# A two-layer decoder trunk on one core: ordering the vector work of the down projection, and its first leftover tile by weight rows

## The chip, the cores and the metric

The kernel runs on one core of one Trainium2 chip. The metric is the device time of one execution in microseconds (us); the time before is the median of three runs. TensorE (PE in the profile) multiplies into eight PSUM banks, VectorE (DVE) and ScalarE (ACT) read those banks, GpSimd (POOL) works from SBUF only, and SyncE (SP) issues most DMAs. Each engine works through its own queue in order and waits on semaphores for the others.

## The reference

A decoder trunk over 1040 tokens (16 meta tokens and 1024 of the input), width 1024, two layers. Layer 0 is a state-space mixer, layer 1 an attention over keys and values that are projected once; each is followed by a convolutional gated feed-forward block. The parts that matter here, cut from the reference:

```python
def _conv_ffn(u, w_up, conv_w, conv_b, w_down):
    h = _causal_dwconv(u @ w_up, conv_w, conv_b)
    g, val = jnp.split(h, 2, axis=-1)
    return (jax.nn.silu(g) * val) @ w_down
...
        if layer < n_a:
            h = h + _ssd_mixer(_rmsnorm(h, ssd_norm[layer]), ...)
        else:
            if layer == n_a:
                kv = _rmsnorm(h, kv_norm) @ w_kv
            ...
            h = h + o @ sb_w_o[j]
        h = h + _conv_ffn(_rmsnorm(h, ffn_norm[layer]), ffn_w_up[layer], ffn_conv_w[layer],
                          ffn_conv_b[layer], ffn_w_down[layer])
    return _rmsnorm(h, final_norm)[:, N_META:]
```

The feed-forward width is 2816, which is 22 rows of 128 weights in the down projection.

## The kernel before

Every float32 product is made of three fast matmuls (`mm3`, L168): each operand is split into a high part (a ScalarE copy) and a low part (the operand minus the high part, on VectorE or GpSimd), and high by high, high by low and low by high are added up in PSUM. So each operand costs one ScalarE and one subtraction before TensorE can use it.

The stages follow one another: mixer, output projection (`out_proj`), entry to the feed-forward block (`enter_ffn`), up projection (`up`), down projection (`down`), attention (`attention`), its projection (`o_proj`), and the second feed-forward block. Outside the attention and part of the mixer, a planner at build time sets each engine's order: it walks through the program with its own durations, and puts an instruction that it thinks is ready ahead of an earlier one that it thinks is not. Inside `manual_schedule` blocks (the attention, L1565) the order is that of the program.

**The down projection** (`down`, L993) runs once per layer. Its first 16 weight rows are multiplied by a seven-product scheme for 2x2 blocks: in each of two rounds the seven products come in the order 1, 2, 7, 6, 5, 3, 4 (L1077), each in two halves (x = 0, 1), so there are 28 steps. `make(n)` (L1133) prepares the operands of step n one step ahead by `Set.operands` (L1033). For products 7, 6, 5 and 3 a weight difference is formed in place, for 7, 6, 5 and 4 a token difference (L1039 to L1050, all on VectorE). Then come the high part of the weights on ScalarE (L1054), their low part on GpSimd (L1055), the high part of the tokens on ScalarE (L1056) and their low part on VectorE (L1057). The buffers of the token parts are of a pool of 28 (`qp`), of which some three steps' worth are free. A step is 48 matmuls in layer 0 (two token tiles of 260 columns, four output blocks) and 24 matmuls of 512 columns in layer 1. A finished product is moved out of its PSUM banks by `add` (L1099): L1103 on ScalarE for some products of the first round, L1105 on VectorE for the others. In the kernel before, only the differences of product 7 are tied to something: they stand behind the last instruction of the up projection (`behind_up`).

The last six weight rows are plain products, four token tiles (j = 0 to 3) by eight output blocks f (L1172 to L1186). `accumulate` (L396) runs all six rows into one bank and adds the bank to h on VectorE (L403); its banks come from a cycle of five. The seven products are put together by 28 VectorE additions (`sums`, L1069, L1074), two of which are asked for behind each block of tile 0. `weights` (L1110; L1113 on ScalarE, L1114 on GpSimd) and `tokens` (L1117; L1124, L1125) prepare the operands.

**The entry to layer 0's feed-forward block**: `out_proj` (L728) adds the last four rows of the mixer's projection inside `enter_ffn`, in four token tiles. Their right-hand operands are split for both halves of the tokens (`split_half`, L185; L189 on ScalarE, L190 on VectorE) before the first tile.

**The last normalization of layer 0**: `norm` (L249) is called for three token tiles; it splits h (L273, L274), adds up squares (`square_sum`, L231) and calls `rstd` (L198), which sums over partitions by two matmuls with a matrix of ones (L204) and makes the factors on ScalarE and VectorE (L207 to L212). The attention then begins with the projections of keys and queries (`half`, L1231) of tiles 0 and 1.

Of the kernel before, what the change touches and what calls it, by code (L numbers as in the profile page):

```python
# [8 lines left out]
F32 = mybir.dt.float32  # L9
# [4 lines left out]
P = 128  # L14
D = 1024
KD = D // P
# [9 lines left out]
HALO = 4  # L26
# [34 lines left out]
PAIRS = 8  # L61
# [25 lines left out]
class Trunk:  # L87
# [161 lines left out]
    def norm(self, h, j, u):  # L249

        s0, n = TT[j]
        if u is None:
            u = [(self.Q("uh", F32R), self.Q("ul", F32R)) for _ in range(KD)] + [self.rp.tile([P, QW], F32, tag="r", name=self.nm("r"))]
        rows = [h[k][:, s0 : s0 + n] for k in range(KD)]
        for k in range(KD):
            self.parts(rows[k], u[k], s0, n, None, self.nc.gpsimd if (j, k) in LPOOL else self.nc.vector)
        self.rstd(self.square_sum(rows, n, D), n, D, u[KD][:, HALO + s0 : HALO + s0 + n], j == 0)
        return u

    def scaled_project(self, w, u, j, q=None, bank=None):  # L260
# [467 lines left out]
    def out_proj(self, hd, ys, yd, pool):  # L728

        a = self.a  # L730
        h = [None] * KD
        for g in range(3):
            ops = [self.split(ys[g][q] if yd[g] is None else self.fetch(yd[g][q], "y"), "y") for q in range(4)]
            for f in range(KD):
                w = self.load_w(a["w_out_f"][g, f], 4 * P)
                if g == 0:
                    h[f] = self.fetch(hd[f], "h", front=HB)
                for s0, n in TT:
                    self.accumulate(h, f, s0, n, lambda i, f: (w[0][:, i * P : i * P + P], w[1][:, i * P : i * P + P]), ops, HB)
        half = lambda x: [self.split_half(ys[3][q][:, L // 2 * x : L // 2 * (x + 1)], "y") for q in range(4)]  # L740
        first = half(0)
        ws = [self.load_wd(a["w_out"][12 + i], i < 2) for i in range(4)]
        return self.enter_ffn(0, h, [(ws, first), (ws, half(1))], pool)

    def load_wd(self, src, row):

# [2 lines left out]
    def enter_ffn(self, layer, h, last, pool):  # L749


        nc, g = self.nc, FFN[layer]
        FN, S = g.tile, g.half
        r = self.rp.tile([P, QW], F32, tag="r", name=self.nm("r"))
        if not g.lead:
            nc.gpsimd.tensor_copy(r[:, :HB], self.zero[:, :HB])
        d = self.dp.tile([KD, P, g.n], F32, tag=f"hm{layer}", name=f"hm{layer}")
        banks = cycle((self.mm, self.lg, self.ex, self.mm, self.lg))
        ms = {}

        def tile(j, work):
            ws, ops = last[j // 2]
            ms[j] = self.sm("ms")
            for f in range(KD):
                self.accumulate(h, f, *g.span(j), lambda i, f: (ws[i][0][:, f * P : f * P + P], ws[i][1][:, f * P : f * P + P]), ops, HB, next(banks), g.part(j // 2)[0])
                self.square_row(ms[j], h, f, *g.span(j))
                next(work, None)

        def factors(j):

            s0, n = g.span(j)
            c = r[:, HB + s0 : HB + s0 + n]
            b, ps = self.tmp("y")[:, :n], ms.pop(j)[:, :n]
            if j % 2 == 0:
# [12 lines left out]
        def form_tiles():  # L787

            out = {}

            def own(i):
                hl = self.Q("bh", F32R), self.Q("bl", F32R)
                out[i] = [tuple(x[:, k * FW : k * FW + HB + FN] for x in hl) for k in range(KD // 2)]

            def wide():
                wide = [(self.Q("bh", F32R), self.Q("bl", F32R)) for _ in range(KD // 4)]

                for x in wide[1]:
# [12 lines left out]
        w0 = self.up_weights(layer, 0, pool)  # L811
        ws0 = next(w0)
        for j in (0, 1):
            tile(j, iter(()))
            factors(j)
        store(0)
        forms = [form_tiles()]
        work = self.forms(layer, h, r, 0, forms[0], pool)
        for j in (2, 3):
            tile(j, work)  # L820
            factors(j)
        store(1)
        for _ in work:
            pass
        return d, ws0 + next(w0), forms, rest()
# [167 lines left out]
    def down(self, layer, gd, hd, pool, after, each=None):  # L993
# [3 lines left out]
        nc, a = self.nc, self.a  # L997
# [8 lines left out]
            nosync = mybir.DependencyInfo(mybir.DependencyClass.NoSync, mybir.DependencyReason.DATA)  # L1006
            self.tc.add_manual_dep(ins.ins, other.ins.name, nosync, reason=reason)

        def behind_up(ins):

            behind(ins, self.last_up, "behind the up projection")

        def pair(t, w):
            return t[:, : 2 * w].rearrange("p (q c) -> p q c", q=2)
# [1 line left out]
        class Set:  # L1016
# [16 lines left out]
            def operands(me, i):  # L1033

                b, w = me.b, me.w
                b11, b12, b21, b22 = b[0, 0], b[0, 1], b[1, 0], b[1, 1]
                a11, a12, a21, a22 = w[0, 0], w[0, 1], w[1, 0], w[1, 1]
                if i == 7:
                    behind_up(tt(a21, a11, a21, op=SUB))  # L1039
                    behind_up(tt(b12, b22, b12, op=SUB))  # L1040
                elif i == 6:
                    tt(a21, a22, a21, op=SUB)
                    tt(b11, b11, b12, op=ADD)
                elif i == 5:
                    tt(a11, a11, a21, op=ADD)
                    tt(b12, b22, b11, op=SUB)
                elif i == 3:
                    tt(a21, a12, a21, op=SUB)
                elif i == 4:
                    tt(b11, b21, b11, op=SUB)  # L1050
                x, y = {1: (b11, a11), 7: (b12, a21), 6: (b11, a21), 5: (b12, a11), 3: (b22, a21), 4: (b11, a22), 2: (b21, a12)}[i]
                gh, gl = (pair(self.Q(z, F32R), QW // 2)[:, :, :S] for z in ("gh", "gl"))
                wh, wl = (self.wp.tile([P, 1024], F32R, tag=z, name=self.nm(z)) for z in ("wh", "wl"))
                nc.scalar.activation(wh, y, AF.Copy)  # L1054
                pt(wl, y, wh.bitcast(F32), op=SUB)  # L1055
                nc.scalar.activation(gh, x, AF.Copy)  # L1056
                tt(gl, x, gh.bitcast(F32), op=SUB)  # L1057
                return gh, gl, wh, wl

        kinds = (self.mm, self.sm, self.lg, self.sm, self.mm, self.sm, self.lg, self.ex)  # L1060
# [110 lines left out]
        res, work = None, sums()  # L1171
        for j in range(4):  # L1172
            out = h if j > 1 else h[:4] + h22
            for f in range(KD):
                self.accumulate(out, f, FN * j, FN, lambda i, f: (ws[i][0][:, f * P : f * P + P], ws[i][1][:, f * P : f * P + P]), us[j // 2], bank=next(banks), base=S * (j // 2))
                for _ in range(2 if j == 0 else 1):
                    next(work, None)
                if j == 3 and each:
                    each(h, f)
            if j == 0:  # L1180
                tokens(1)
            else:
                if j == 1:
                    for f in range(4):
                        tt(acc[5, f], acc[5, f], h22[f], op=ADD)
                res = after(h, j - 1, res)  # L1186
# [184 lines left out]
    def attention(self, u, pool):  # L1371
# [30 lines left out]
        for kind, j in (("k", 0), ("q", 0), ("k", 1), ("q", 1)):  # L1402
            for h in range(2):
                for f in first.half(kind, j, h):
                    f()
        self.token_factors(u[KD], pool)
        for p in range(PAIRS):
            prev = None
# [24 lines left out]
    def o_proj(self, hd, od, pool):  # L1433
# [24 lines left out]
                self.accumulate(h, f, *g.span(j), lambda i, f: (w[0][:, i * P : i * P + P], w[1][:, i * P : i * P + P]), ops[j // 2], HB, base=-g.lead)  # L1458
        ops = [part(p, 0) for p in range(first, PAIRS)]
        ws = [self.load_wd(a["w_o"][first - 2 + i], i < 2) for i in range(4)]  # L1460
        return self.enter_ffn(1, h, [(ws[2:], ops), (ws, [part(p, 1) for p in range(first - 2, PAIRS)])], pool)


    def finish(self, h, j):
# [168 lines left out]
```

## Time and profile before

| what | value |
|---|---|
| median of three runs | 2992.21 us (2991.93 to 2997.83) |
| the profiled execution | 2995.8 us, span of its instructions 2994.1 us |
| granted TensorE clock, mean | 0.983 |
| TensorE busy | 2879.0 us, 96% |
| VectorE busy | 2304.0 us, 77% |
| ScalarE, GpSimd busy | 1653.4 us, 1308.0 us |

In the span of the profiled execution, layer 0's entry to the feed-forward block begins at about 837 us, its down projection runs from about 1363 to 1614 us, the attention from there to about 2165 us, and layer 1's down projection from about 2735 us to the end. A wait's row names the engine and line that waited, what it waited for, the sum in us, the number of waits, and the longest.

### The profile page before, as it was taken

How to read it: one execution, taken by the hardware profiler on the slowest of the kernel's cores; microseconds unless marked ns; L12 is line 12 of the kernel's file. 1: busy time of each engine (PE TensorE's matmuls, PEld its weight loads, DVE VectorE, ACT ScalarE, POOL GpSimd, SP SyncE). 2: the span in 40 equal slices, each digit the busy share in tenths (PEclk: the TensorE clock that was granted, in tenths of full speed). 3: DMA queues.
4: the chain of work that ended last, by engine and by line, in shares of the span. 5: the costliest groups of instructions: out<-in, count | busy, mean ns of one | idle time of the engine just before them, and what ended most of it. 6: DMA issues, size and time to landing. Idle time of an engine off the chain costs nothing.

```text
span 2994.1 us, 57318 instructions
## 1 busy us (share of the span) xinstructions
PE 2879.0 (96%) x21863; PEld 2738.0 (91%) x21863; DVE 2304.0 (77%) x4026; ACT 1653.4 (55%) x3403; POOL 1308.0 (44%) x1250
## 2 busy tenths in 40 slices
PE   7999999989998999999999999999899999999998
PEld 4999898879998999998999999999798999998878
DVE  5586868885369887878876888888839878878785
ACT  4555555553245555555334788887736555554433
POOL 1254444442334666663442222222342766764451
PEclk9999999999999999999999999999999999999999
DMA  5233333323122222224232122221331222225321
GB/s 162 70 107 90 106 89 105 106 70 139 63 80 72 79 73 84 79 86 177 74 130 86 55 61 66 64 70 54 106 141 57 80 84 78 75 82 176 106 99 64
DMA packets 123411, 272.72 MB, mean 91 GB/s; under 512 B 13664, under 2 KB 53216, under 8 KB 123136
## 3 DMA queue, kind: packets, MB, share of 16 engines
q1 hardware_dynamic: 117760, 257.93, 26.6%
q10 hardware_dynamic: 4112, 6.56, 0.7%
q0 software_dynamic: 1264, 4.57, 0.4%
q8 instruction: 172, 2.82, 0.4%
q14 instruction: 103, 0.84, 0.1%
HBM read 200.89 MB, written 53.20 MB: 85 GB/s over the span
## 4 chain that ended last, share of the span: by engine, by line
PE 77%; DVE 12%; issue 4%; ACT 3%; POOL 2%; DMA 2%; SPq 0%; DVEq 0%; ACTq 0%; POOLq 0%
PE p L172 9%; PE p L171 9%; PE p L173 9%; PE acc L172 6%; PE acc L171 6%; PE acc L173 6%; PE pj L171 6%; PE pj L172 6%; PE pj L173 6%; PE po L1366 3%; PE lg L1325 3%; PE wT L1352 2%; DVE D L598 1%; PE ms L831 1%; DVE xbc L545 1%
## 5 line engine op out<-in xcount | busy, mean ns | idle before, releaser
L171 PE MATMUL pj<-uh,wh 128*128 128x348 f32 (+2 forms) x1536 | 507.0, 330 | 11.7 <-ACT bk L629 5.9
L172 PE MATMUL pj<-ul,wh 128*128 128x348 f32 (+2 forms) x1536 | 499.7, 325 | 0.0
L173 PE MATMUL pj<-uh,wl 128*128 128x348 f32 (+2 forms) x1536 | 496.3, 323 | 0.0
L171 PE MATMUL p<-bh,fh 128*128 128x262 f32 (+1 forms) x1408 | 403.5, 287 | 7.7 <-ACT c L293 2.8
L173 PE MATMUL p<-bh,fl 128*128 128x262 f32 (+1 forms) x1408 | 402.6, 286 | 3.6 <-POOL fl L905 3.6
L172 PE MATMUL p<-bl,fh 128*128 128x262 f32 (+1 forms) x1408 | 402.3, 286 | 0.1
L905 POOL TENSOR_TENSOR fl<-x,fh 128x1024 fp32r<-128x1024 f32 x88 | 212.4, 2414 | 267.4 <-ACT fh L904 217.7
L172 PE MATMUL p<-bl,wh 128*128 128x262 f32 (+1 forms) x1056 | 302.0, 286 | 6.1 <-DVE bl L857 6.1
L171 PEld LDWEIGHTS pj<-uh,wh 128*128 128x128 f32 x1536 | 292.8, 191 | 16.2 <-ACT xbc L293 4.3
L171 PE MATMUL p<-bh,wh 128*128 128x262 f32 (+1 forms) x1056 | 302.8, 287 | 0.9 <-ACT bh L856 0.9
L173 PE MATMUL p<-bh,wl 128*128 128x262 f32 (+1 forms) x1056 | 301.9, 286 | 0.0
L165 POOL TENSOR_TENSOR wl<-w,wh 128x1024 fp32r<-128x1024 f32 (+2 forms) x76 | 155.7, 2050 | 318.7 <-ACT wh L164 318.7
L172 PEld LDWEIGHTS pj<-ul,wh 128*128 128x128 f32 x1536 | 293.2, 191 | 1.8 <-issue 1.0
L173 PEld LDWEIGHTS pj<-uh,wl 128*128 128x128 f32 x1536 | 292.7, 191 | 0.8 <-issue 0.8
L296 DVE SCALAR_TENSOR_TENSOR c<-p,params,c 128x260 f32<-128x260 f32 (+1 forms) x528 | 249.8, 481 | 54.6 <-ACT c L293 45.1
L171 PEld LDWEIGHTS p<-bh,fh 128*128 128x128 f32 x1408 | 270.2, 192 | 8.6 <-ACT c L293 6.0
L173 PEld LDWEIGHTS p<-bh,fl 128*128 128x128 f32 x1408 | 269.4, 192 | 4.1 <-POOL fl L905 4.0
L172 PEld LDWEIGHTS p<-bl,fh 128*128 128x128 f32 x1408 | 270.2, 192 | 0.6 <-DVE bl L857 0.5
L947 DVE TENSOR_TENSOR c<-c,c 128x260 f32<-128x260 f32 (+1 forms) x176 | 245.0, 1394 | 5.5 <-ACT c L943 2.4
L952 ACT ACTIVATE ft<-p 128x262 f32<-128x262 f32 (+1 forms) x352 | 127.4, 384 | 203.8 <-DVE p L955 177.0
L1055 POOL TENSOR_TENSOR wl<-w,wh 128x1024 fp32r<-128x1024 f32 x56 | 148.9, 2662 | 205.4 <-ACT wh L1054 195.7
L171 PE MATMUL acc<-gh,wh 128*128 128x260 f32 (+1 forms) x672 | 215.0, 323 | 10.9 <-DVE h L1105 7.2
(325 smaller groups left out, 8472.7 us busy)
## 6 DMA issues: line engine op xcount, KB each, us to landing
w<-in_w_up SPq DMA_DIRECT2D x88, 512.0 KB
w<-in_w_down SPq DMA_DIRECT2D x44, 512.0 KB
w<-in_w_in SPq DMA_DIRECT2D x40, 512.0 KB
E<-ea_d SPq DMA_DIRECT2D x32, 464.0 KB
D<-acs_d SPq DMA_DIRECT2D x32, 420.5 KB
g<-c SPq DMA_DIRECT2D x88, 130.0 KB
g<-c SPq DMA_DIRECT2D x88, 128.0 KB
b<-g SPq DMA_DIRECT2D x16, 520.0 KB
```

The lines of the kernel that those rows point to most:

```text
L165: nc.gpsimd.tensor_tensor(wl[:, :n], w32[:, :n], wh[:, :n].bitcast(F32), op=ALU.subtract)
L171: mm(out, wh, uh, start=first, stop=False, skip_group_check=joins)
L172: mm(out, wh, ul, start=False, stop=False, skip_group_check=joins)
L173: mm(out, wl, uh, start=False, stop=last, skip_group_check=joins)
L296: nc.vector.scalar_tensor_tensor(out, ps[:, o + i : o + i + n], wcol(i), out, op0=ALU.mult, op1=ALU.add)
L905: tt(lo[:, :n], t, hi[:, :n].bitcast(F32), op=ALU.subtract)
L947: self.last_up = tt(g[:, :FN], g[:, :FN], v[:, :FN], op=ALU.mult)
L952: nc.scalar.activation(s[:, :N], ps[:, :N], AF.Copy)
L1055: pt(wl, y, wh.bitcast(F32), op=SUB)
L1325: nc.tensor.matmul(ps[:nt, :m], part[:, c0 : c0 + nt], ks[a][:, s0 : s0 + m], start=x == 0, stop=x == 1)
L1352: nc.tensor.transpose(pt[:ns, x * CB : x * CB + nt], bt[a][:nt, x * CB : x * CB + ns], self.ident[:nt, :nt])
L1366: nc.tensor.matmul(po[64 * a : 64 * a + 64, :nt], v[: CH[c][1], c, 64 * a : 64 * a + 64], wt[a][: CH[c][1], c, :nt], start=x == 0, stop=x ...
```

## The change

There are four edits.

1. In `Set.operands` each weight difference of a step is tied behind the low part of the tokens (L1057) two steps in front, each token difference behind that of the step in front. The tie (`behind`) orders the two on VectorE's queue and adds no semaphore. The differences of product 7 also keep their tie to the up projection.
2. Plain tile 0 of `down` runs by weight rows: row 0 for all eight output blocks into eight banks, then row 1, and so on. The eight additions to h come after, with two `sums` behind each as before. Tiles 1 to 3 keep the order by output blocks.
3. `norm` for tile 2 leaves its `rstd` to the attention, which calls it behind the key projection of tile 0.
4. `enter_ffn` takes its operands as functions. In layer 0 the second half's splits are issued behind tile 0's products. In layer 1 the operands are made beforehand, as they were.

```diff
@@ norm
-        self.rstd(self.square_sum(rows, n, D), n, D, u[KD][:, HALO + s0 : HALO + s0 + n], j == 0)
+        sums = self.square_sum(rows, n, D)
+        factors = lambda: self.rstd(sums, n, D, u[KD][:, HALO + s0 : HALO + s0 + n], j == 0)
+        if j < 2:
+            factors()
+        else:
+            self.late_factors = factors
@@ out_proj
-        return self.enter_ffn(0, h, [(ws, first), (ws, half(1))], pool)
+        return self.enter_ffn(0, h, [(ws, lambda: first), (ws, lambda: half(1))], pool)
@@ enter_ffn
+        operands(0)
         for j in (0, 1):
             tile(j, iter(()))
+            if j == 0:
+                operands(1)
             factors(j)
@@ down
-        def behind_up(ins):
-
-            behind(ins, self.last_up, "behind the up projection")
+        lows = []
+
+        def behind_low(ins, n):
+
+            if len(lows) >= n:
+                behind(ins, lows[-n], "behind the low part in front")
...
+                a = {7: (a21, a11, a21, SUB), 6: (a21, a22, a21, SUB), 5: (a11, a11, a21, ADD), 3: (a21, a12, a21, SUB)}.get(i)
+                b = {7: (b12, b22, b12, SUB), 6: (b11, b11, b12, ADD), 5: (b12, b22, b11, SUB), 4: (b11, b21, b11, SUB)}.get(i)
+                for x, n in ((a, 2), (b, 1)):
+                    if x:
+                        d = tt(*x[:3], op=x[3])
+                        behind_low(d, n)
+                        if i == 7:
+                            behind(d, self.last_up, "behind the up projection")
...
-                tt(gl, x, gh.bitcast(F32), op=SUB)
+                lows.append(tt(gl, x, gh.bitcast(F32), op=SUB))
...
+            wide_first = [bank("acc") for bank in kinds] if j == 0 else []
+            for i, (hi, lo) in enumerate(us[0] if j == 0 else ()):
+                for f, ps in enumerate(wide_first):
+                    wh, wl = (w[:, f * P : f * P + P] for w in ws[i])
+                    self.mm3(ps[:, :FN], wh, wl, hi[:, :FN], lo[:, :FN], i == 0, i == len(ws) - 1)
             for f in range(KD):
-                self.accumulate(out, f, FN * j, FN, ..., us[j // 2], bank=next(banks), base=S * (j // 2))
+                if j == 0:
+                    tt(out[f][:, :FN], out[f][:, :FN], wide_first[f][:, :FN], op=ADD)
+                else:
+                    self.accumulate(out, f, FN * j, FN, ..., us[j // 2], bank=next(banks), base=S * (j // 2))
@@ attention
+            if (kind, j) == ("k", 0):
+                self.late_factors()
@@ o_proj
-        return self.enter_ffn(1, h, [(ws[2:], ops), (ws, [part(p, 1) for p in range(first - 2, PAIRS)])], pool)
+        second = [part(p, 1) for p in range(first - 2, PAIRS)]
+        return self.enter_ffn(1, h, [(ws[2:], lambda: ops), (ws, lambda: second)], pool)
```

More of the change, by code (lines that the diff above doesn't have):

```diff
@@ L758, in enter_ffn, with operands @@
         banks = cycle((self.mm, self.lg, self.ex, self.mm, self.lg))
-        ms = {}
+        ms, made = {}, {}
+        def operands(x):
+            made[x] = last[x][0], last[x][1]()
         def tile(j, work):
-            ws, ops = last[j // 2]
+            ws, ops = made[j // 2]
             ms[j] = self.sm("ms")
@@ L1037, in operands @@
                 a11, a12, a21, a22 = w[0, 0], w[0, 1], w[1, 0], w[1, 1]
[L1038 to L1050, printed above, removed]
+                a = {7: (a21, a11, a21, SUB), 6: (a21, a22, a21, SUB), 5: (a11, a11, a21, ADD), 3: (a21, a12, a21, SUB)}.get(i)
[6 more added lines that the diff above has]
+                            behind(d, self.last_up, "behind the up projection")
                 x, y = {1: (b11, a11), 7: (b12, a21), 6: (b11, a21), 5: (b12, a11), 3: (b22, a21), 4: (b11, a22), 2: (b21, a12)}[i]
@@ L1173, in down @@
             out = h if j > 1 else h[:4] + h22
+            wide_first = [bank("acc") for bank in kinds] if j == 0 else []
[3 more added lines that the diff above has]
+                    self.mm3(ps[:, :FN], wh, wl, hi[:, :FN], lo[:, :FN], i == 0, i == len(ws) - 1)
             for f in range(KD):
-                self.accumulate(out, f, FN * j, FN, lambda i, f: (ws[i][0][:, f * P : f * P + P], ws[i][1][:, f * P : f * P + P]), us[j // 2], bank=next(banks), base=S * (j // 2))
+                if j == 0:
+                    tt(out[f][:, :FN], out[f][:, :FN], wide_first[f][:, :FN], op=ADD)
+                else:
+                    self.accumulate(out, f, FN * j, FN, lambda i, f: (ws[i][0][:, f * P : f * P + P], ws[i][1][:, f * P : f * P + P]), us[j // 2], bank=next(banks), base=S * (j // 2))
                 for _ in range(2 if j == 0 else 1):
```

## The prediction

> **What bounds the kernel now.** I read the page first: shares of the span and the chain that ended last.
>
> ```profile
> span 2994.1 us, 57318 instructions
> PE 2879.0 (96%) x21863; PEld 2738.0 (91%) x21863; DVE 2304.0 (77%) x4026; ACT 1653.4 (55%) x3403; POOL 1308.0 (44%) x1250
> PE 77%; DVE 12%; issue 4%; ACT 3%; POOL 2%; DMA 2%; SPq 0%; DVEq 0%; ACTq 0%; POOLq 0%
> ```
>
> TensorE is busy 96% of the span and the change removes no matmul, so all there is to win is TensorE's idle time, 2994.1 - 2879.0 = 115 us over the whole kernel, and the stretches in which its clock is cut. I therefore asked next what TensorE waits for in the stages that the change touches. First layer 0's down projection with the step into the attention (1350 to 1640 us), then layer 1's down projection (2730 us to the end), then the entry to layer 0's feed-forward block (830 to 920 us).
>
> ```profile
> PE acc L171 <- DVE h L1105: 7.2, 3, 4.9
> PE acc L171 <- DVE h L403: 2.6, 1, 2.6
> PE acc L171 <- DVE p L1105: 2.3, 1, 2.3
> PE ms L204 <- DVE sq L245: 2.2, 1, 2.2
> ...
> PE acc L172 <- DVE gl L1057: 0.7, 1, 0.7
> ```
>
> ```profile
> PE acc L172 <- DVE gl L1057: 5.1, 1, 5.1
> PE acc L171 <- DVE h L403: 2.3, 1, 2.3
> PE acc L173 <- POOL wl L1055: 1.7, 1, 1.7
> PE acc L173 <- POOL wl L1114: 1.5, 1, 1.5
> PE acc L171 <- DVE h L1105: 0.3, 1, 0.3
> ```
>
> ```profile
> PE acc L171 <- DVE h L403: 3.4, 1, 3.4
> ```
>
> Nearly all of these are waits for VectorE: for a bank that an addition has not emptied (L1105, L403), or for a low part (L1057). The third view gives busy times, matmul counts (in brackets) and the clock (the column after POOL) by stretch. The last four rows are the two rounds of each down projection.
>
> ```profile
> 825.00:850.00 25.00, 21.57 (x155) 21.06 (x154) 12.16 (x15) 8.03 (x13) 17.27 (x10) 1.00 0.20 73
> 1600.00:1625.00 25.00, 22.02 (x145) 20.61 (x144) 16.88 (x27) 11.47 (x24) 13.65 (x10) 0.86 0.22 76
> 2895.00:2920.00 25.00, 20.92 (x138) 19.18 (x137) 22.55 (x33) 6.94 (x9) 10.51 (x5) 0.95 0.31 106
> 2920.00:2945.00 25.00, 25.00 (x211) 25.00 (x211) 18.15 (x35) 6.15 (x14) 2.32 (x2) 0.98 0.07 22
> ...
> 1363.00:1457.00 94.00, 86.30 (x697) 85.52 (x697) 78.02 (x69) 42.35 (x65) 40.76 (x16) 0.96 0.40 134
> 1457.00:1540.00 83.00, 79.07 (x658) 78.65 (x657) 65.93 (x82) 32.57 (x36) 42.42 (x17) 1.00 0.26 88
> 2735.00:2820.00 85.00, 79.87 (x333) 64.13 (x332) 70.55 (x50) 38.02 (x47) 39.93 (x15) 0.96 0.41 145
> 2820.00:2901.00 81.00, 79.26 (x342) 63.54 (x341) 70.07 (x58) 32.35 (x35) 42.62 (x16) 1.00 0.20 68
> ```
>
> A wait costs twice where the clock falls behind it: 0.04 of 94 us is 3.8 us lost in the first round of layer 0, 0.04 of 85 us is 3.4 us in that of layer 1. A matmul of 260 columns takes 25.00 / 211 = 0.118 us of TensorE (fourth row).
>
> **Edit 1, the ties.** VectorE's timeline shows what stands in front of the low part for which TensorE waits 5.1 us in layer 1, and in front of the addition for which it waits 4.9 us in layer 0; below them GpSimd and ScalarE.
>
> ```profile
> 2743.69 3.43 DVE L1040 TENSOR_TENSOR b<-b,b 128x1024 f32<-128x1024 f32 x1
> 2747.05 3.44 DVE L1039 TENSOR_TENSOR w<-w,w 128x1024 f32<-128x1024 f32 x1
> ...
> 2751.54 4.52 DVE L1043 TENSOR_TENSOR b<-b,b 128x1024 f32<-128x1024 f32 x2
> ...
> 2757.12 1.21 DVE L1057 TENSOR_TENSOR gl<-b,gh 128x1024 fp32r<-128x1024 f32 x1
> ...
> 1390.30 3.37 DVE L1045 TENSOR_TENSOR w<-w,w 128x1024 f32<-128x1024 f32 x1
> 1393.59 0.75 DVE L1105 TENSOR_TENSOR h<-h,acc 128x260 f32<-128x260 f32 x2
> ...
> 2746.82 2.58 POOL L1055 TENSOR_TENSOR wl<-w,wh 128x1024 fp32r<-128x1024 f32 x1 [0.78 <-ACT wh L1054]
> 1377.87 2.99 ACT L1056 ACTIVATE gh<-b 128x1040 fp32r<-128x1040 f32 x3
> ```
>
> Differences of products 7 and 6 run before the low part of product 2, and one of product 5 before product 2's additions. A VectorE operation of two SBUF operands takes 1.21 us alone, and 3.4 us where it meets GpSimd's low part (2747.05 beside 2746.82), 2.2 us more. With the ties, product 6's token difference (L1043) can't pass product 7's low part, nor a difference of product 5 that of product 6. In layer 0 this removes the waits of 4.9 and 0.7 us and the 3.8 us of clock, 9.4 us; in layer 1 the 5.1 and the 3.4 us, 8.5 us. The work for the two starts fits: VectorE is at 78.0 of 94 and 70.6 of 85 us. Sum 17.9 us, from 0 (the planner finds other work to put there) to 17.9.
>
> The differences don't vanish; they move towards their use. In 1400 to 1457 us VectorE now does some of the second round's in advance:
>
> ```profile
> L1040 DVE TENSOR_TENSOR b<-b,b 128x1040 f32<-128x1040 f32 x2 | 4.5, 2268 | 2.5 <-DMA b<-g 2.3 <-PE acc L172 0.2
> L1043 DVE TENSOR_TENSOR b<-b,b 128x1040 f32<-128x1040 f32 x2 | 2.5, 1236 | 0.0
> L1039 DVE TENSOR_TENSOR w<-w,w 128x1024 f32<-128x1024 f32 x2 | 2.4, 1218 | 4.3 <-DMA w<-in_w_down 4.3
> ```
>
> Six operations, 6 x 1.22 = 7.3 us alone or 6 x 2.27 = 13.6 us beside GpSimd, go into the second round. There VectorE has 65.9 us of work against 79.1 us of TensorE's in layer 0, 70.1 against 79.3 in layer 1. At 7.3 us both fit, with 5.9 and 1.9 us to spare. At 13.6 us layer 0 is 0.4 us over and layer 1 4.4 us. Against it, the later differences of that round (products 5, 3, 4) can no longer go ahead of additions, which is what its waits of 2.3 + 2.3 us in layer 0 are. I take a loss of 2.0 us, between a gain of 4.6 and a loss of 8.3 (4.8 us over, and 3.5 us of clock).
>
> **Edit 2, the first plain tile by rows.** The same 144 matmuls, 17.1 us; a row is 24 matmuls, 2.8 us. In layer 1 the tile's waits are 1.5 us for the weights' low part (L1114), 0.3 and 2.3 us for banks, with 0.05 x 25 = 1.25 us of clock; in layer 0 2.6 us for a bank (L403). By rows, row i is needed 2.8 x i us later and no bank is needed twice, so these go: 5.3 and 2.6 us. VectorE's timeline of layer 0 shows what the banks' additions stand behind.
>
> ```profile
> 1541.71 5.10 DVE L1074 TENSOR_TENSOR p<-p 128x520 f32<-128x520 f32 x4
> 1546.74 1.91 DVE L1074 TENSOR_TENSOR h<-h,p 128x520 f32<-128x520 f32 x3
> ...
> 1552.84 0.74 DVE L403 TENSOR_TENSOR h<-h,acc 128x260 f32<-128x260 f32 x2
> ```
>
> What is late next is tile 1. Its first three banks are those of blocks 0, 4 and 7, which end 2.5 us, 1.1 us and 0 us before the tile does. An addition takes 0.37 us, one of the `sums` 0.64 us. If one sum stands between each two additions, block 7's bank is free 8 x 0.37 + 8 x 0.64 = 8.1 us after block 0 ended, 5.6 us after the tile; tile 1 needs it after two blocks of 18 matmuls, 4.3 us: a wait of 1.3 us. With the 16 sums of the program's order all in front it is 8 x 0.37 + 16 x 0.64 - 2.5 - 4.3 = 6.4 us. With half of them done during the tile, which VectorE has time for, between these and zero. I take 1.0 us in each layer.
>
> **Edit 4, the late split (layer 0 alone).** The 3.4 us wait at 840 us is for a bank whose addition stands behind two splits:
>
> ```profile
> 838.30 5.23 DVE L190 TENSOR_TENSOR y<-xbc,y 128x520 fp32r<-128x520 f32 x2
> 843.46 1.75 DVE L403 TENSOR_TENSOR h<-h,acc 128x260 f32<-128x260 f32 x5
> ```
>
> Behind tile 0 the second half's splits have the time of tile 1 before tile 2 needs them, so they cost nothing there: 12.2 of 25 us are VectorE's there. Gain 3.4 us; its least is 0, if tile 0's operands meet GpSimd as before.
>
> **Edit 3, the late factors.** TensorE waits 2.2 us for the sum of squares, then runs its two matmuls. But the key projection's third matmul needs GpSimd's low part, which is little earlier:
>
> ```profile
> 1615.53 2.35 POOL L1217 TENSOR_TENSOR wl<-w,wh 128x1024 fp32r<-128x1024 f32 x1 [0.41 <-ACT wh L1216]
> ...
> 1618.32 1.51 PE ms L204 x2
> ```
>
> GpSimd ends at 1617.88, the matmuls on the squares start at 1618.32: 0.4 us are won, and the cut clock (0.86 in 1600 to 1625) stays. The factors' four VectorE operations, two on ScalarE and two matmuls stand behind the keys of tile 0 and in front of queries and keys of tile 1; the transposed factors need them only after three more projections. Bounds: 0 and 2.2 + 3.5 us.
>
> One weighing of the clock. The wait of 3.4 us leaves the clock at 1.00 (825 to 850), while 2.3 us behind 1.5 and 0.3 us bring 0.95 (2895 to 2920). The Trainium skill, "TensorE: Matmul & The Clock Gate", section "Why this matters for your kernels", asks for no idle gap above some 3 us and blames one whole idle window. By that the 1.25 us of clock would not be counted and the sum would be that much smaller; the rows show that several short waits do it too, so I keep it.
>
> **The sum.** 17.9 - 2.0 + (5.3 + 2.6 - 2.0) + 3.4 + 0.4 = 25.6 us. The planner lays everything behind an edit anew, and VectorE meets GpSimd in other places: I take off two such meetings on the path, 2 x 2.2 = 4.4 us. That leaves 21.2 us. The profiled execution, 2995.8 us, would come to 2974.6; it lies 3.6 us above the median, so the median goes from 2992.2 to 2971.0 us. This case's own range is 2961 to 2981 us.
>
> **Rivals.**
> *The second rounds pay.* The moved differences meet GpSimd each time (2268 ns): 4.8 us over and 3.5 us of clock as above, and the starts keep half of the 17.9 us because the ties also hold VectorE idle there. 25.6 - 4.4 - 6.3 - 9.0 = 5.9 us (2986), with the starts whole 14.9 us (2977); I put it at 2983 us, between them. For it: 70.1 of 81 us in layer 1. Against: VectorE has idle time in every round.
> *The first tile's banks come too late.* The 16 sums stand in front, 6.4 us in each layer: edit 2 turns from 5.9 us into 7.9 - 12.8 = -4.9, the time is 2982 us; with the clock cut behind both (7 us) 2989. For it: in layer 0 11 us of sums and splits did stand before the first addition. The Trainium skill, same page, section "Loop structure matters more than you think", advises to finish one output tile over all its weight rows before the next, which edit 2 gives up.
> *Slower: VectorE's queue blocks at the ties.* Each difference now stands behind a low part that waits for its high part and that for a buffer. Low part, difference, ScalarE's high part and next low part are 1.21 + 1.21 + 1.0 + 1.21 = 4.6 us in a row, of a step of 48 x 0.118 = 5.7 us. One meeting with GpSimd (2.2 us) makes it 1.1 us too long, and additions queue behind it, which hold banks. There are 10 such steps in each of 4 rounds; the gain of 21.2 us is gone at 0.53 us a step. At 0.8 us it is 32 - 21 = 11 us slower, 3003 us. Against: about three steps' buffers lie between VectorE and TensorE, so the chain may lag for a while without a wait.
> *No effect.* The ties are hints to a planner that may find its waits elsewhere: 2992, within 6 us.
>
> **How the numbers follow.** A measurement tells about 0.2%, 6 us, from no change. Chances: the sum 0.50; second rounds 0.13; late banks 0.10, of which 0.02 lie within 6 us; blocked ties 0.15; no effect 0.12, of which 0.08 within 6 us and 0.02 on each side. Faster 0.50 + 0.13 + 0.08 + 0.02 = 0.73, same 0.10, slower 0.17. The range from 2959 to 2994 leaves out the slower cases and some 0.03 below.
>
> **What would show it.** Right: in both first rounds no wait above 2 us for L1057 or L1105, and clock 1.00; L1043 behind product 7's L1057; no wait for L403 or L1114 in tile 0; at the entry no wait for L403; the low part of the keys, not L245, as the wait at the attention's start. Wrong: waits for L1105 or L1057 in the second rounds of over 6 us in sum, a wait for the additions of tile 0 at tile 1's start above 3 us, or ScalarE's high parts as VectorE's waits in every step.

## The result, and the profile after

| | before | after |
|---|---|---|
| time, median us (lowest to highest, runs) | 2992.07 (2991.28 to 2997.83, 4) | 2980.16 (2977.91 to 2980.81, 4) |
| ratio to before, 95% interval | | 0.9954 [0.9942, 0.9965] |
| profiled execution, its span, us | 2995.8, 2994.1 | 2979.88, 2977.8 |

The medians lie 11.9 us apart, 0.40% (the ratio in the table, taken over all runs, gives 0.46%), where 21.2 us were forecast: right in its direction and inside the range, about half in size. From the page of the kernel after:

```profile
span 2977.8 us, 57315 instructions
PE 2871.6 (96%) x21863; PEld 2732.0 (92%) x21863; DVE 2304.7 (77%) x4026; ACT 1647.6 (55%) x3403; POOL 1309.9 (44%) x1250
PE 77%; DVE 11%; issue 3%; ACT 3%; POOL 3%; DMA 2%; SPq 0%; ACTq 0%; DVEq 0%; POOLq 0%
```

The same matmuls are there (21863); TensorE's busy time fell by 7.4 us (its mean granted clock is 0.987 instead of 0.983), and its idle time from 115 to 106 us. That makes 16 us and not 11.9, because the profiled execution of the kernel before lay 3.7 us above its median. Line numbers have moved: the additions L1105 are now L1114, the low parts L1057 L1066, all differences L1056, the entry's and plain tiles' additions L403 L408 (tile 0's L1190), GpSimd's low part L1055 is L1064.

TensorE's waits in the kernel after (us in total, times, longest): entry to layer 0's block, then layer 0's first round, its second round with the plain tiles and the attention's start, layer 1's first round, and the rest.

```profile
PE acc L171 <- DVE h L408: 4.9, 2, 3.8
...
PE acc L171 <- DVE h L1114: 1.6, 1, 1.6
...
PE acc L171 <- DVE p L1114: 4.0, 3, 1.8
PE pj L173 <- POOL wl L1234: 1.8, 1, 1.8
PE pj L171 <- ACT wh L1233: 1.3, 1, 1.3
PE acc L171 <- DVE h L1114: 0.8, 1, 0.8
...
PE acc L172 <- DVE gl L1066: 1.0, 1, 1.0
...
PE acc L171 <- DVE h L1114: 4.4, 2, 4.0
```

Busy time by stretch, with the clock in the column after POOL: the entry, layer 0's two rounds, layer 1's two rounds (which end 17 us earlier than in the kernel before), and layer 1's first plain tile.

```profile
825.00:850.00 25.00, 20.14 (x138) 19.66 (x137) 13.86 (x15) 9.29 (x14) 17.62 (x10) 0.93 0.18 66
1363.00:1457.00 94.00, 90.93 (x757) 90.56 (x757) 74.31 (x71) 44.50 (x70) 43.77 (x17) 1.00 0.42 145
1457.00:1540.00 83.00, 78.13 (x638) 76.75 (x637) 74.11 (x91) 32.08 (x35) 43.81 (x18) 1.00 0.29 94
...
2727.00:2806.00 79.00, 77.98 (x336) 62.84 (x335) 67.60 (x48) 37.14 (x47) 41.18 (x15) 1.00 0.44 155
2806.00:2884.00 78.00, 78.00 (x337) 63.06 (x336) 71.29 (x61) 31.79 (x34) 40.24 (x16) 1.00 0.20 68
2880.00:2905.00 25.00, 20.56 (x134) 19.25 (x133) 18.32 (x26) 5.26 (x7) 10.97 (x5) 0.86 0.29 106
```

The first rounds are much as forecast: where TensorE waited 4.9 and 5.1 us it now waits 1.6 and 1.0 us, and the clock is 1.00 in both. Two waits were not forecast: the entry's, which was 3.4 us and is now 4.9 with a clock of 0.93 instead of 1.00, and a new one of 4.4 us in layer 1's first plain tile, where the clock is 0.86.

VectorE's timeline of the kernel after shows what stands in front of the awaited addition, first at the entry, then in that plain tile:

```profile
839.53 5.24 DVE L190 TENSOR_TENSOR y<-xbc,y 128x520 fp32r<-128x520 f32 x2
844.69 1.75 DVE L408 TENSOR_TENSOR h<-h,acc 128x260 f32<-128x260 f32 x5
...
2881.60 1.87 DVE L1114 TENSOR_TENSOR h<-h,acc 128x512 f32<-128x512 f32 x3
2888.70 0.69 DVE L1134 TENSOR_TENSOR g<-g 128x512 fp32r<-128x512 f32 x1 [5.23 <-ACT g L1133]
2889.31 0.68 DVE L1114 TENSOR_TENSOR h<-h,acc 128x512 f32<-128x512 f32 x1
```

and ScalarE's what VectorE stood idle for 5.23 us for, the high part of a token block that a DMA delivered late:

```profile
2888.04 0.63 ACT L1133 ACTIVATE g<-g 128x512 fp32r<-128x512 f32 x1 [2.33 <-DMA g<-g]
```

So the late split (edit 4) was moved in the program but not on VectorE: two splits (L190) still run in front of the first additions. And in layer 1 the addition that frees a bank of product 4 queues behind a low part of the second half's tokens (`tokens(1)`), which waits for a transfer.

The table gives the length of each stage, from its first matmul in the trace to that of the next, in us of the profiled execution of each kernel (the last column ends with the span). The experiments' rows are explained below.

| kernel | entry, tile 0 to the first `ms` | L0 products | L0 plain tiles to attention | L1 products | L1 plain tiles to the end |
|---|---|---|---|---|---|
| before | 10.6 | 176.3 | 75.8 | 166.3 | 93.3 |
| after | 13.7 | 171.3 | 72.8 | 157.3 | 93.7 |
| e1 ties only | 13.7 | 171.2 | 77.2 | 157.3 | 94.9 |
| e2 no rows | 12.4 | 172.5 | 77.4 | 157.3 | 94.4 |
| e5 split tied | 7.1 | 171.5 | 72.8 | 157.3 | 93.9 |
| e6 tokens tied | 12.1 | 172.2 | 72.7 | 157.3 | 88.0 |
| e7 both tied | 7.1 | 171.5 | 72.8 | 157.3 | 87.9 |
| e8 ties, first round | 12.5 | 178.2 | 72.8 | 165.6 | 91.0 |
| e9 ties, second round | 14.0 | 178.3 | 72.7 | 162.3 | 93.7 |
| e10 ties, product 7 | 12.5 | 177.2 | 72.9 | 167.4 | 90.9 |
| e12 both tied, no rows | 7.1 | 171.4 | 77.8 | 157.3 | 91.6 |

### The profile page after: what moved, and what is told of

Same layout as the page of the kernel before. It is cut to its first block, busy times and chain, and to the rows that moved or that the text cites. A ratio compares the mean times of both kernels' runs of the same rounds, so it can differ in the third digit from the quotient of the medians.

```text
span 2977.8 us, 57315 instructions
## 1 busy us (share of the span) xinstructions
PE 2871.6 (96%) x21863; PEld 2732.0 (92%) x21863; DVE 2304.7 (77%) x4026; ACT 1647.6 (55%) x3403; POOL 1309.9 (44%) x1250
## 3 DMA queue, kind: packets, MB, share of 16 engines
q8 instruction: 172, 2.82, 0.4%
## 4 chain that ended last, share of the span: by engine, by line
PE 77%; DVE 11%; issue 3%; ACT 3%; POOL 3%; DMA 2%; SPq 0%; ACTq 0%; DVEq 0%; POOLq 0%
PE p L173 9%; PE p L172 9%; PE p L171 9%; PE acc L171 6%; PE acc L172 6%; PE acc L173 6%; PE pj L171 6%; PE pj L172 6%; PE pj L173 6%; PE po L1383 3%; PE lg L1342 2%; PE wT L1369 2%; DVE gl L1066 1%; PE ms L842 1%; DVE D L603 1%
## 5 line engine op out<-in xcount | busy, mean ns | idle before, releaser
L1064 POOL TENSOR_TENSOR wl<-w,wh 128x1024 fp32r<-128x1024 f32 x56 | 151.4, 2706 | 190.3 <-ACT wh L1063 184.5
```

## The experiments: each edit by itself

**e1: the ties alone.** The kernel before, with the change in `operands` and nothing else:

```
-                if i == 7:
-                    behind_up(tt(a21, a11, a21, op=SUB))
...
+                for x, n in ((a, 2), (b, 1)):
+                    if x:
+                        d = tt(*x[:3], op=x[3])
+                        behind_low(d, n)
```

> The kernel before with edit 1 alone (the ties). Theory A (the stages add up, as the trace of the whole change reads): the ties are worth the waits that they removed in both down projections, 8.1 us in layer 0 and 9.2 us in layer 1, and the other edits together cost some 3 us. Then this kernel is at 2992 - 17 = 2975 us, faster than the whole change (2980), with the first plain tile's old waits (2.6 us in layer 0, some 5 us with the clock in layer 1) still there. Rival B (each edit makes the planner lay out everything anew, and the gain belongs to no single edit): ties alone give 6 us or less, 2986 us or more.

Measured: 2984.48 us (2979.82 to 2990.69), ratio 0.9976 [0.9966, 0.9987], between the two theories. By stage the ties are worth 9.0 us in layer 1's products, where theory A had 9.2, and 5.1 us in layer 0's, where it had 8.1: 14.1 together. What takes part of that back is outside them: the entry, which this kernel's code leaves alone, is 13.7 us instead of 10.6, and the plain tiles are 1.4 and 1.6 us longer. Rival B's reason is not what the traces show: in e1 and in the kernel before, TensorE, VectorE, ScalarE and GpSimd run the same operations (by kind and tile name) in the same order everywhere but in the products. What differs at the entry is when GpSimd's low parts meet VectorE's splits. The first two rows are of the kernel before, the others of e1:

```profile
835.54 2.42 DVE L190 TENSOR_TENSOR y<-xbc,y 128x520 fp32r<-128x520 f32 x2 [0.71 <-ACT y L189]
837.35 5.63 POOL L905 TENSOR_TENSOR fl<-x,fh 128x1024 fp32r<-128x1024 f32 x2
...
830.81 4.16 DVE L190 TENSOR_TENSOR y<-xbc,y 128x520 fp32r<-128x520 f32 x2 [0.71 <-ACT y L189]
831.52 5.68 POOL L912 TENSOR_TENSOR fl<-x,fh 128x1024 fp32r<-128x1024 f32 x2
```

GpSimd starts its two low parts 1.8 us behind the first split in the kernel before and 0.7 us behind it in e1, and the first two splits take 4.16 us instead of 2.42. TensorE's wait of 3.4 us becomes two, of 1.1 and 3.8 us, and the clock is halved for 3.4 us. In the plain tiles TensorE's waits are close to those of before (2.6 us in layer 0 in both, 4.7 against 4.1 us in layer 1), but a half clock of 3.4 us stands behind layer 0's, where there was none, and two behind layer 1's, where there was one. The clock in e1 behind the entry's wait, and behind that of layer 0's plain tile:

```profile
840.80:844.20 3.40, 3.29 (x15) 3.29 (x16) 1.68 (x6) 1.66 (x5) 0.67 (x1) 0.50 0.45 154
1547.40:1550.80 3.40, 3.40 (x18) 3.40 (x17) 3.40 (x8) 0.00 (x0) 0.00 (x0) 0.50 0.01 2
```

**e2: without the rows.** The kernel after, its tile 0 by output blocks as before:

```
-            wide_first = [bank("acc") for bank in kinds] if j == 0 else []
...
-                if j == 0:
-                    tt(out[f][:, :FN], out[f][:, :FN], wide_first[f][:, :FN], op=ADD)
-                else:
-                    self.accumulate(...)
+                self.accumulate(...)
```

> The whole change without edit 2 (plain tile 0 by output blocks again). Theory A: edit 2 won some 1.8 us in layer 0 and lost some 2.5 us in layer 1, where TensorE waited 4.4 us for banks 1.9 us into the tile and lost 3.5 us of clock; so 2979 to 2981 us, the same as the whole change. The prediction's own term (5.9 us gained by rows): 2986 us. Rival B: anything, with new waits outside the tile.

Measured: 2984.92 us (2980.72 to 2990.74), ratio 0.9980 [0.9971, 0.9989]. Some 5 us are lost, so theory A (rows worth nothing) falls. By stage the rows save 4.6 us in layer 0 and 0.7 in layer 1. Of the 4.6 us, e2's wait for a bank is 2.8 and a half clock of 3.4 us behind it 1.7; the kernel before had such a wait (2.6 us) without the half clock.

**e3 and e4: without the late split, without the late factors.**

```
-        return self.enter_ffn(0, h, [(ws, lambda: first), (ws, lambda: half(1))], pool)
+        second = half(1)
+        return self.enter_ffn(0, h, [(ws, lambda: first), (ws, lambda: second)], pool)
```

> The whole change without edit 4 (both halves' splits issued before the entry's tile 0 in layer 0, as before). Theory A: edit 4 cost 1.4 us more of waits and 1.7 us of clock, some 2.5 us at the beginning of the up projection; so 2977.5 us, with the entry's one wait of 3.4 us back. The prediction's term (3.4 us gained by edit 4): 2983.5 us.

```
-        if j < 2:
-            factors()
-        else:
-            self.late_factors = factors
+        factors()
...
-            if (kind, j) == ("k", 0):
-                self.late_factors()
```

> The whole change without edit 3 (the third tile's factors made inside the normalization again). Theory A and the prediction agree within what can be told: edit 3 is worth between -0.4 and +0.4 us, 2980 us; TensorE waits for the squares 2.2 us in place of 1.8 us for the low part of the keys. A gain of 2 us or more for edit 3 (2982 us) would speak for the clock: one cut slice of 3.4 us in place of two.

Measured: e3 2979.41 us (2976.23 to 2985.81), ratio 0.9963 [0.9950, 0.9975]; e4 2978.06 us (2975.42 to 2982.73), ratio 0.9961 [0.9948, 0.9973]. Both are the kernel after within its interval: neither edit does anything that can be measured. e3's entry wait is 3.7 us. At the attention's start e4 has the waits of before again:

```profile
PE ms L204 <- DVE sq L245: 2.2, 1, 2.2
PE pj L171 <- ACT wh L1228: 0.7, 1, 0.7
```

2.9 us in sum, against 1.8 + 1.3 = 3.1 us in the kernel after. The late factors exchange one wait for another.

## The experiments: the two waits that were left

**e5: the second half's split, tied.** The kernel after, with each of the four low parts of that split behind tile 0's last addition on VectorE. (Lines from here are up to 5 higher in e5 and e7.)

```
+        d = self.nc.vector.tensor_tensor(lo, t, hi.bitcast(F32), op=ALU.subtract)
+        if other is not None:
+            self.tc.add_manual_dep(d.ins, other.ins.name, nosync, reason="behind the first tile")
...
+        self.last_acc = self.nc.vector.tensor_tensor(h[f][:, o], ...)
...
+        return self.enter_ffn(0, h, [(ws, lambda: first), (ws, lambda: half(1, self.last_acc))], pool)
```

> The kernel after, with the four low parts of the second half's split also tied behind the last addition of tile 0 at the entry to layer 0's feed-forward block. Theory A (the late split failed only because VectorE's order was not changed by it: the splits still stand in front of the first addition): the entry wait of 1.1 + 3.8 us goes, with up to 1.7 us of clock, and nothing is late at tile 2; about 2975 us, the mark of the entry's last matmul 5 us earlier. Rival B (the four low parts then run behind tile 0 in a row, 4 x 1.2 us or more, in front of the additions of tile 1, which hold banks): the wait goes to tile 1 or 2 at 3 to 4 us, 2980 us.

Measured: 2971.25 us (2969.87 to 2973.15), ratio 0.9927 [0.9915, 0.9940]; 9 us below the kernel after, more than theory A asked. VectorE's timeline, and the entry's busy times:

```profile
842.94 0.43 DVE L411 TENSOR_TENSOR h<-h,acc 128x260 f32<-128x260 f32 x1 [3.21 <-PE acc L173]
843.28 4.71 DVE L190 TENSOR_TENSOR y<-xbc,y 128x520 fp32r<-128x520 f32 x4
847.91 0.75 DVE L411 TENSOR_TENSOR h<-h,acc 128x260 f32<-128x260 f32 x2
```

```profile
825.00:850.00 25.00, 25.00 (x186) 24.53 (x185) 11.84 (x21) 11.84 (x21) 20.48 (x12) 1.00 0.16 54
```

The four splits run behind the last addition of tile 0, in 4.71 us; in the kernel after two of them took 5.24 us, beside GpSimd. TensorE is busy for all of 25.00 us. The entry falls from 13.7 to 7.1 us, 6.6 of the 9; the rest I have not placed (the stretch ahead of the entry is 3.7 us shorter in this execution, with the same code). The 6.6 is of one execution of each: kernels with the entry of the kernel after stand between 12.1 and 14.0 us in the table.

**e6: the second half's tokens, tied.** The kernel after, with the low parts of `tokens(1)` behind the last addition of the products:

```
-                tt(lo, lo.bitcast(F32), hi.bitcast(F32), op=SUB)
+                d = tt(lo, lo.bitcast(F32), hi.bitcast(F32), op=SUB)
+                if x:
+                    behind(d, self.last_add, "behind the products")
```

> The kernel after, with the low parts of the second half's tokens in the plain tiles (tokens(1)) tied behind the last addition of the products, in both layers. Theory A (the 4.0 us wait in the first row of layer 1's plain tile stood there because product 4's additions queued behind a low part that waited for a token transfer): in layer 1 that wait falls below 1 us and the clock in 2880 to 2905 us goes from 0.86 to 0.96 or more, 4 to 7 us less, 2973 to 2976 us; layer 0, where the products' last additions met no such low part, unchanged. Rival B (eight banks in 2.8 us are more than VectorE's additions at 0.4 to 0.7 us can free, whatever stands between): a wait of 2 to 3 us stays there, 2978 to 2980 us.

Measured: 2974.70 us (2970.49 to 2975.63), ratio 0.9937 [0.9924, 0.9949], theory A. In e6 VectorE runs six additions in a row where one had waited, and the clock in the tile is whole:

```profile
2884.91 3.66 DVE L1114 TENSOR_TENSOR h<-h,acc 128x512 f32<-128x512 f32 x6
```

```profile
2880.00:2905.00 25.00, 24.82 (x178) 22.86 (x178) 25.00 (x33) 6.69 (x9) 12.11 (x5) 1.00 0.31 106
```

Layer 1's end falls from 93.7 to 88.0 us, layer 0 stays (72.7).

**e7: both.** The edits of e5 and e6 together.

> The kernel after with both of the ties of the two runs before this one. Theory A: their gains add, 2968 to 2971 us, below both kernels. Rival B: each is relaid by the planner as a whole, so the sum is not their sum, 2976 to 2980 us.

Measured: 2965.82 us (2965.05 to 2967.84), ratio 0.9910 [0.9897, 0.9924]: 14 us below the kernel after, and the fastest here. The gains add (6.6 + 5.8 us by stage). Its waits in the entry's stretch and from 2820 us on no longer name a bank for more than 1.3 us.

**e12: both, without the rows.** e7 with the edit of e2.

> The kernel with both added ties, its first plain tile by output blocks over two banks again, as in the kernel before. Theory A (the order by rows and the tied tokens each remove a wait of their own: the rows those for the weights' low part and for a bank in both layers, the tie the one that the eight banks brought in layer 1): 3 us back in layer 0 as with the rows alone, 3 to 6 us in layer 1, 2971 to 2975 us. Rival B (in layer 1 the tied tokens alone free the bank in time, so that the rows are worth only layer 0's 3 to 4.5 us there): 2968 to 2971 us.

Measured: 2974.77 us (2973.01 to 2980.55), ratio 0.9942 [0.9929, 0.9956]: theory A. The rows are worth 9 us here, 5.0 in layer 0 and 3.7 in layer 1. In e12's end the weights' low part is waited for again:

```profile
PE acc L173 <- POOL wl L1126: 2.9, 2, 2.1
```

**e11: both, without the late factors.** e7 with the edit of e4.

> The kernel with both added ties (the second half's split and the second half's tokens), without the late factors of the third tile. Theory A (the late factors change nothing that can be measured, as alone): 2964 to 2968 us. Rival B (with the other waits gone, the sum of squares at the attention's start is worth its 2.2 us and the clock behind it, up to 3.4 us): 2968 to 2971 us.

Measured: 2966.33 us (2964.32 to 2970.56), ratio 0.9921 [0.9908, 0.9935]. Theory A: still nothing.

## The experiments: which ties work

The kernel after, with a condition on `behind_low(d, n)`; `me.k` is 0 or 2 in the first round and 4 or 6 in the second:

```
e8:   if me.k < 4:
e9:   if me.k >= 4:
e10:  if me.k >= 4 and i == 7:
```

> The kernel after with the ties of the differences in the first round of each down projection alone; the second round's differences are free, as in the kernel before. Theory A (second rounds cost what the prediction took, 2 us, in layer 0's four waits of 1.5, 0.7, 1.8 and 0.8 us): about 2978 us, with the same first rounds. Rival B (second rounds pay: the ties there are the loss): 2972 us or less, VectorE's busy time in 1457 to 1540 us back from 74 to 66 us. Rival C (the second round's free differences are again taken in advance into the end of the first round, in front of its low parts and additions): half of the gain of the ties goes, 2984 to 2987 us.

> The kernel after with the ties of the differences in the second round of each down projection alone; the first round's are free. Ties in the first round alone gave next to nothing (2988.8 us). Theory A (what the ties remove is VectorE standing idle for a transfer in front of additions, when a difference of the second round is taken in advance): all of the ties' gain is here, 2978 to 2982 us, and no wait above 2 us for an addition in 1400 to 1457 us. Rival B (each round's ties serve its own low parts, half of the gain each): 2984 to 2986 us, and in layer 1's first round the wait of about 5 us for a low part behind product 6's difference is back.

> The kernel after with the ties of product 7's differences in the second round alone: four of the second round's 14 differences in each layer, the first to touch the quarters that are loaded anew; all later differences of a set need their results. Theory A (it is these that wait for transfers in VectorE's queue): as all ties of the second round, 2978 to 2982 us. Rival B (the order in every step counts): 2985 us or more.

Measured: e8 2988.83 us (2984.24 to 2994.21), ratio 0.9988 [0.9978, 0.9997]; e9 2989.47 us (2985.27 to 2996.07), 0.9992 [0.9981, 1.0004]; e10 2987.93 us (2981.48 to 2992.60), 0.9995 [0.9984, 1.0005]. Either half of the ties alone is worth next to nothing: the products of both layers together are 1.2 us longer than before in e8, 2.0 us shorter in e9 and 2.0 us longer in e10. Both halves together are worth 14 us there. (The times hold the other three edits too, and no run has those without any tie, so the stages decide.) e8 is its rival C at full strength, or slightly beyond. The theory that I formed on it, that the second round's ties do it all, fell with e9 and e10. TensorE's waits for additions in e8's first round in layer 0, and what VectorE does at its end (1429 to 1442 us):

```profile
PE acc L171 <- DVE h L1115: 7.5, 2, 5.9
```

```profile
1429.56 1.22 DVE L1056 TENSOR_TENSOR w<-w,w 128x1024 f32<-128x1024 f32 x1
1432.41 2.82 DVE L1056 TENSOR_TENSOR b<-b,b 128x1040 f32<-128x1040 f32 x1 [1.65 <-issue]
1435.16 3.38 DVE L1067 TENSOR_TENSOR gl<-b,gh 128x1040 fp32r<-128x1040 f32 x1
1438.46 2.42 DVE L1115 TENSOR_TENSOR h<-h,acc 128x260 f32<-128x260 f32 x7
1442.47 1.24 DVE L1056 TENSOR_TENSOR b<-b,b 128x1040 f32<-128x1040 f32 x1 [1.59 <-DMA b<-g]
```

With the second round free, its differences are taken in advance into the last products of the first. There a difference of 2.82 us, an idle time of 1.65 us in front of it, whose cause the profile does not show, and a low part of 3.38 us beside GpSimd stand ahead of seven additions. With the first round free (e9), that round's own differences stand in front again. TensorE's waits in e9 in the two first rounds, and VectorE's queue in layer 0:

```profile
PE acc L171 <- DVE h L1115: 5.0, 1, 5.0
PE acc L172 <- DVE gl L1067: 0.7, 1, 0.7
...
PE acc L172 <- DVE gl L1067: 4.3, 1, 4.3
```

```profile
1396.26 3.36 DVE L1056 TENSOR_TENSOR w<-w,w 128x1024 f32<-128x1024 f32 x1
1399.54 0.74 DVE L1115 TENSOR_TENSOR h<-h,acc 128x260 f32<-128x260 f32 x2
```

These are the 4.9 and 0.7 us of the kernel before, at the same steps, and 4.3 us where it had 5.1. So in layer 0 there are two places where a difference can block the additions, and each set of ties clears one. e8 holds the first round's start clear and pays at its end; e9 the reverse. In layer 1 e8 has no wait of that size: its products are as long as before (165.6 against 166.3 us) with five waits of 0.7 to 1.8 us, for low parts of tokens and for parts of the weights.

## Why the prediction was right, and where it was wrong

**Edit 1, the ties: the mechanism is shown, the size nearly.** Product 6's difference now runs behind product 7's low part, and first-round waits above 2 us are gone. VectorE in the kernel after: the last low part of product 7 and the first token difference of product 6 in layer 1, then what is left in front of the awaited additions in layer 0.

```profile
2753.59 3.01 DVE L1066 TENSOR_TENSOR gl<-b,gh 128x1024 fp32r<-128x1024 f32 x1
2756.53 1.21 DVE L1056 TENSOR_TENSOR b<-b,b 128x1024 f32<-128x1024 f32 x1
...
1388.51 3.43 DVE L1056 TENSOR_TENSOR w<-w,w 128x1024 f32<-128x1024 f32 x1
1391.86 2.09 DVE L1114 TENSOR_TENSOR h<-h,acc 128x260 f32<-128x260 f32 x6
```

17.9 - 2.0 = 15.9 us were forecast for both products, 5.0 + 9.0 = 14.0 are there. Two terms of layer 0 are mis-sized. The wait of 4.9 us was to go whole; 1.6 us of it stay, behind a weight difference of 3.43 us, which a tie to the low part two steps in front lets through. And the clock: I charged the whole cut, 3.8 us (6.8 us at half are 3.4; the rest is the rounding of 0.04), beside the wait; but the clock falls during the wait. The kernel before in steps of 2 us:

```profile
1388.00:1390.00 2.00, 1.20 (x10) 0.99 (x9) 2.00 (x3) 0.88 (x1) 0.00 (x0) 1.00 0.00 0
1390.00:1392.00 2.00, 0.00 (x0) 0.00 (x0) 2.00 (x2) 0.17 (x1) 1.75 (x1) 0.95 0.00 0
1392.00:1394.00 2.00, 0.00 (x0) 0.00 (x0) 2.00 (x3) 0.00 (x0) 0.59 (x1) 0.50 0.00 0
1394.00:1396.00 2.00, 1.85 (x8) 1.88 (x9) 2.00 (x4) 0.00 (x0) 0.00 (x0) 0.50 0.03 8
...
1398.00:1400.00 2.00, 2.00 (x16) 2.00 (x16) 2.00 (x5) 0.39 (x1) 0.00 (x0) 0.84 0.00 0
```

TensorE stops at 1389.2 and is back at 1394.15 (1.20 and 1.85 us busy in those rows); the half clock lasts from about 1391.8 (0.95) to 1398.6 (0.84): only 4.5 us of it, half lost, cost anything, 2.2 us. (In layer 1 it is 5.6 of 6.8 us, 2.8 us where 3.4 were charged.) What the prediction did not have is that the ties work only as a set. Its chance for "no effect" rested on a planner that finds its waits elsewhere; e8 and e9 show that this happens whenever one of the two places is left open.

**The second rounds did not pay.** VectorE's load in layer 0's rose from 65.9 to 74.1 us of 83. TensorE's four waits there are 4.8 us where two of 1.6 and 2.3 had been (the prediction counted 2.3 + 2.3, but 0.7 us of that stands in the first round): 0.9 us more, inside the bounds. In layer 1 the wait of 1.7 us for L1055 is gone. The rival at 2983 us fell. So did the slower one: TensorE's waits in the products name no high part, and VectorE waits for one in 7 of layer 0's 28 steps and 6 of layer 1's (5 and 5 before), not in every step.

**Edit 2, the rows: right in layer 0, wrong in layer 1.** Forecast were 1.6 us net in layer 0 and 4.3 in layer 1; against before there are 3.0 and -0.4. The wait at tile 1's start, the 1.0 us in each layer, did not come. The step that failed is "no bank is needed twice, so these go". It looked at the banks behind the tile and not at those in front: eight banks are asked for within one row, 2.8 us, and product 4 still held some. With the tokens tied (e6, e7) layer 1's end is 5.4 us shorter than before: more than the 4.3 us forecast, since the tie and the rows each remove a wait there.

**Edit 4, the late split: wrong.** The 3.4 us of gain became nothing by time (e3). I read "behind tile 0" in the program's order as "behind tile 0" in VectorE's queue; the order is laid by a planner, and only the ties bind it. My least for this edit was 0, for a meeting with GpSimd; it should have named this cause, which in edit 1 I had taken as given. Bound (e5), the entry gains 6.6 us against the kernel after, and 3.5 against before, which is the 3.4 forecast. That the entry of the kernel after is 3.1 us longer than before is not this edit's doing: in e3, without it, it is 12.2 us, and in e1 13.7.

**Edit 3** was put at 0.4 us; nothing can be measured, as forecast, and the low part of the keys (with the high part in front) is the wait in place of L245.

**The planner's share.** I took off 4.4 us because the planner lays everything behind an edit anew. It did not: the ties (e1) changed no engine's order outside the products. Without that term the sum was 25.6 us. With its two loose ends tied (e7) the change gives 0.9910, which is 27 us (23 to 31) of its own runs of before, and by stage 3.5 + 4.8 + 3.0 + 9.0 + 5.4 = 25.7 us. That the totals agree so closely is in part luck: edit 1's products give 13.8 us of the 15.9, and the plain tiles, with the tokens' tie, 8.4 where 5.9 were forecast. The miss of 9.3 us lies mostly at the entry (3.1 us longer where edit 4 was to save 3.4) and in layer 1's share of edit 2.

**Not settled.** Whether the longer entry comes with the ties or with the execution that was profiled. It is not VectorE's queue: e1 has the order of before there, and the kernel after and e6, whose engines run the same order up to the plain tiles, stand at 13.7 and 12.1 us, with 4.11 and 2.51 us for the first two splits. But e1 saves 7.7 us by its median of 11 runs, against 14.1 in the products of its profile, so more than one execution may lose there. The clock's part of it, as of the stretch ahead, differs between the profiled executions.

## What to carry to other kernels

Where a planner orders an engine's queue, a move in the program text is not a move in the queue: look at the timeline of that engine after each edit, and bind the order where it matters. A dependency that is bound at one place lets filler in at the next, so bind every place where an operation that waits for a transfer can stand ahead of one that frees a bank. An order over eight banks needs all eight at its start: trace who frees the last of them, and what that work queues behind.

## What the runs showed of the hardware that was not expected

A TensorE wait and the clock cut behind it can overlap: with a wait of 4.95 us in the kernel before the half clock began about 2.6 us into it, so that 2.3 of its 6.8 us cost nothing, and the cut was not a second price of its own full length. Nor is it the same each time: behind the same wait of 4.95 us in e9 the half clock began 4.7 us into it and lasted 3.4 us, a loss of 1.6 us instead of 2.2. A wait of 3.4 us at 840 us in the kernel before left the clock at 1.00; one of 3.5 us in its place in e2 halved it for 3.4 us, and two of 1.1 + 3.8 us brought 0.93 over 25 us in the kernel after. A wait of 2.6 us in layer 0's plain tile left it at 1.00 in the kernel before and halved it for 3.4 us in e1. So the length of a wait alone does not tell here whether the clock falls.

The work ahead of the entry, which no edit touches, ended between 831.5 and 837.8 us in the profiled executions of these kernels. Differences of a few us between two single profiles are therefore read by stage, not from their spans.
